# Transformer blocks on one core: row vectors and normalized x through TensorE, attention values as the stationary side, two heads side by side

## The chip, the core and the metric

The kernel runs on one core of a Trainium2 chip. The metric is the device time of one execution in microseconds (us). Engines are named as the profile names them: PE is TensorE's matmul side, PEld its weight loads, DVE VectorE, ACT ScalarE, POOL GpSimd, SP the queue that starts the DMA transfers.

## What is computed

A sequence of 256 tokens of width 1024 in float32 passes through three blocks, cut here to what the change touches:

```python
c_act = silu(c)
for layer in range(2):                          # adaptive layers 0 and 1
    shift, scale, gate = split(c_act @ w_ada[layer] + b_ada[layer], 3)
    h = rms_norm(x, norm_g[layer]) * (1 + scale) + shift
    y = even_mixer(h) if layer == 0 else odd_mixer(h)
    x = x + gate * y
x = rms_norm(x, final_g)

# odd_mixer (layer 1): 16 heads of 64, causal softmax over 256 keys
p = softmax(q @ k.T * scale, causal)
y = (merge(p @ v) * silu(z)) @ w_out

# second block: 8 heads of stick-breaking attention, one of three gated branches
A[t, s] = sigmoid(z_ts) * prod_{s<j<t} (1 - sigmoid(z_tj))
y_a = merge(A @ v) @ w_attn_out
```

The second block goes on with a depthwise convolution branch, a short convolution branch, gates, and a feed-forward layer.

## The kernel before

Everything lives in two token tiles (`tt` 0 and 1) of 128 rows. Each projection is a sum over 8 row blocks of 128 (fewer for the narrow ones). For float32 accuracy at the faster float32r rate, each operand is split into a rounded part and its rest: `split` (line 651) makes the two halves of a weight tile with one copy on ACT and one subtraction on DVE, and `mm3` (line 658) issues three matmuls of 128x512, here called wide matmuls, into an `acc` bank of PSUM. Everything else, scores, values and transposes, is plain float32 and goes to the `m` banks, four of them.

The order of work is written twice. First, `program` records every instruction; a ticker (`after`, `every`) places side work such as attention units between the projection's matmuls. Then `Order.best` and `solve` (lines 271 and 284) list-schedule the recorded instructions with the durations of `cost` (line 508), choose the slots of the pools, and issue all engines' instructions in that order. Each engine then runs its own list strictly in order. `fused` (line 148) keeps the instructions recorded inside it together as one piece of that list.

What the change and the steps below touch:

- **Start.** The condition vector `c` is loaded twice, as columns into `col`, and as a row repeated on 128 partitions into `cb` (line 745; a 512 KB DMA of its own). ACT and DVE apply silu to both. `ada_v` (line 964) multiplies a transposed 512 KB weight tile by `cb` on DVE, summing along the row. For the first two row blocks `ada_pe` (line 971) does this on TensorE, four column tiles of 32 at a time. The results land in `ab`. `rsqrt` makes the norms of x, ACT writes x times its norm into `xn` (line 1005), and `h_t` (line 995) transposes a 128x128 piece of it, applies scale and shift on ACT into `f`, and splits `f` into `hT`. `e1_mm` (line 1020) uses `hT` and the first weights for the first wide matmuls: 12 of 512 columns and 6 of 408 for each of 8 row blocks.
- **Gates.** `gate_rows` (line 1361) turns a column of gate values into a row on all partitions: DVE multiplies the identity by each column (16 tiles over both layers), and TensorE multiplies by `ones`.
- **Layer 1.** `o_unit` (line 1483) works on 4 heads for tt 0 and on 2 for tt 1 through `sm_unit` (line 883): scores, softmax numerators `e`, transposes into `pt`, then `values`: for each head and key block one matmul with `pt` stationary (128x128) and `v` moving (64 columns). That is 48 matmuls. `o_done` divides by the sums, `gated` multiplies by silu(z), `to_lhs` transposes and splits the product.
- **Stick-breaking.** `st_unit` (line 1703) does one head: scores, tanh, a scan on DVE, three transposes, three matmuls for the values, 64 columns moving (24 in all). `st_done` transposes and splits the result, 8 transposes.

Of the kernel before, what the change touches and what calls it, by code (L numbers as in the profile page):

```python
# [21 lines left out]
P = 128  # L22
D = 1024
# [86 lines left out]
_ROWS = [("c", 1024), ("fg", 1024), ("mg", 1024), ("ffg", 1024),  # L110
# [397 lines left out]
def cost(engine, name, writes, reads, kw):  # L508
# [69 lines left out]
def program(ctx: ExitStack, tc: tile.TileContext, found, x_d, wst, rows, cols, rope, w2, out, dbg=None):  # L578
# [167 lines left out]
    for a, b in ((0, 72), (72, NCOL)):  # L746
        nc.sync.dma_start(col[:, a:b], cols[:, a:b])
        if a == 0:
            nc.sync.dma_start(cb, rows[0:1, ROWS["c"][0]:ROWS["c"][1]].to_broadcast([P, D]))
# [7 lines left out]
    ones = const.tile([P, P], F32, name="ones")  # L757
    V.memset(ones, 1.0)
# [124 lines left out]
    def sm_unit(tt, segs, klen, masks, o, den, sink=None):  # L883
# [20 lines left out]
        def turn():  # L904
# [3 lines left out]
            transposes(pt, e.rearrange("p a b -> p (a b)"), nb, s.rearrange("p a b -> p (a b)").rearrange("p (c q) -> p c q", q=P))  # L908

# [451 lines left out]
    def gate_rows(layer, j):  # L1361
# [121 lines left out]
    def o_unit(j, tt, u):  # L1483
        n = 4 if tt == 0 else 2
        segs = []
        for i in range(n):
            h = head(tt, u, i)
            segs.append(([(st["q", j][:, h // 2, tt * P:tt * P + P], st["k", j][h % 2][:, h // 2, 0:P * (tt + 1)])],
                         [st["v", j][:, t, 64 * h:64 * h + 64] for t in range(tt + 1)], h))
        kl = P * (tt + 1)  # L1490
        masks = lambda s: (s[:, :, kl - P:kl], causal[:, None, :].to_broadcast([P, n, P]))
        return sm_unit(tt, segs, kl, masks, lambda sl: get(o1, (j, tt), lambda: bank([P, 8, 64], n="o1"))[:, sl, :],
                       lambda sl: den1[:, j, tt, sl:sl + 1])

    def o_done(j, tt):
# [3 lines left out]
        o = t2([P, 8, 64], n="o")  # L1499
        V.tensor_tensor(o, o1[j, tt], cf[:, :, None].to_broadcast([P, 8, 64]), op=ALU.mult)  # L1500
        o1[j, tt] = o
# [20 lines left out]
    for tt in range(2):  # L1522
        after(1 + tt, lambda tt=tt: gated(o1[0, tt], tt, 0))
# [7 lines left out]
    def mid1():  # L1531
        tk.drain()
        for tt in range(2):
            gated(o1[1, tt], tt, 1)
# [166 lines left out]
    os_ = {}  # L1701

    def st_unit(h):
# [14 lines left out]
        def turn():  # L1718
# [4 lines left out]

            def values():
                o = get(os_, ("p", h // 4), lambda: bank([P, 2, 4, 64], n="os"))
                v = qk["v"][:, :, 64 * h:64 * h + 64]
                PE.matmul(o[:, 0, h % 4, :], at[:, 0:P], v[:, 0, :], start=True, stop=True, skip_group_check=True)
                PE.matmul(o[:, 1, h % 4, :], at[:, P:256], v[:, 0, :], start=True, stop=False, skip_group_check=True)
                PE.matmul(o[:, 1, h % 4, :], at[:, 256:384], v[:, 1, :], start=False, stop=True, skip_group_check=True)
                if h % 4 == 3:  # L1730
                    ob = get(os_, "o", lambda: [t2([P, 8, 64], n="so") for _ in range(2)])
                    for tt in range(2):
                        S.activation(ob[tt][:, h - 3:h + 1, :], o[:, tt], AF.Copy, scale=0.5)
# [4 lines left out]

    ya = new_lhs(4)

    def st_done():
        for tt in range(2):
            to_lhs(ya, os_["o"][tt].rearrange("p h d -> p (h d)"), tt, 0, 4)
# [8 lines left out]
    every(2, 8, [launch(lambda h=h: st_unit(h)) for h in range(8)] + [lambda: None, lambda: None, st_done])  # L1752
# [98 lines left out]
def layout(inputs):  # L1851
# [19 lines left out]
    def pe(v):  # L1871
# [14 lines left out]
        "c": a["c"][0], "fg": a["final_g"], "mg": a["mix_norm_g_2"][0],  # L1886
# [35 lines left out]
```

## Time and profile before

| | |
|---|---|
| median of 3 runs | 759.78 us (757.1 to 760.51) |
| profiled execution, its own time | 761.01 us |
| span of the profile | 759.3 us |
| PE busy | 733.1 us (97%), 3712 instructions |
| PEld busy | 596.4 us (79%) |
| DVE busy | 573.7 us (76%), 1057 instructions |
| ACT busy | 404.1 us (53%), 715 instructions |
| DMA | 148.08 MB, mean 195 GB/s |
| granted TensorE clock | 0.997 |

Busy time of PE is the union of matmuls that overlap in the pipeline, so it is not the work done: a wide matmul lasts 407 ns in the trace, while the next may start much earlier. What a matmul costs in a stream is read from the starts of its neighbours. Nearly all instructions carry line 562, the helper that records them, so groups are told apart by tiles and shapes. A float32 matmul appears as two records (x2 for one matmul), a transpose as one.

### The profile page before, as it was taken

Reading aid. Unit: us, or ns where it says so; the run is one execution under the profiler, and the core shown is the slowest. Engines: PE = TensorE matmul, PEld = TensorE weight load, DVE = VectorE, ACT = ScalarE, POOL = GpSimd, SP = SyncE. Lnnn points to the kernel's source line nnn. Section 1 sums busy time; section 2 is a strip of 40 time slices with the busy share of each in tenths; the row PEclk is TensorE's granted clock in tenths of the full one; section 3 lists DMA queues with packets and bytes.
Section 4 is the critical chain, followed back from the end, with each engine's and each line's share of the span. In section 5 each row is a group of like instructions: output and inputs, shape, how many; then the busy total and the mean of one; then the engine's idle time right before and its main releaser. Section 6 shows DMA issues by size and latency. Waiting matters only on the chain.

```text
span 759.3 us, 10452 instructions
## 1 busy us (share of the span) xinstructions
PE 733.1 (97%) x3712; PEld 596.4 (79%) x3712; DVE 573.7 (76%) x1057; ACT 404.1 (53%) x715; POOL 13.7 (2%) x40
## 2 busy tenths in 40 slices
PE   3999999997999999999999999999999999999998
PEld 1887788786787888878877778878887888888886
DVE  4899899957987564598899999997857555646531
ACT  5565878747454546446455564566445444435420
POOL 1000000000000000001000000000000000000000
PEclk9999999999999999999999999999999999999999
DMA  8998978734684533456532476654747555645101
GB/s 325 400 372 285 368 251 297 236 130 140 210 289 136 196 129 114 148 191 209 182 113 84 139 226 208 206 184 174 250 139 253 191 195 173 214 140 193 57 1 55
DMA packets 43572, 148.08 MB, mean 195 GB/s; under 512 B 6272, under 2 KB 7424, under 8 KB 43520
## 3 DMA queue, kind: packets, MB, share of 16 engines
q1 hardware_dynamic: 43520, 147.41, 56.6%
q8 instruction: 29, 0.48, 0.3%
q14 instruction: 23, 0.19, 0.1%
HBM read 146.34 MB, written 1.05 MB: 194 GB/s over the span
## 4 chain that ended last, share of the span: by engine, by line
PE 76%; DVE 10%; DMA 7%; ACT 5%; issue 1%; SPq 0%; ACTq 0%; DVEq 0%
PE acc L562 65%; PE m L562 11%; DMA k<-in_wst_dram 7%; DVE k L562 5%; DVE kr L562 4%; ACT k L562 3%; ACT kr L562 2%; DVE x L562 1%; SPq L562 0%; DVE tiny L562 0%; DVE ab L562 0%; DVE keepA L562 0%; ACTq L562 0%; DVEq L562 0%
## 5 line engine op out<-in xcount | busy, mean ns | idle before, releaser
L562 PE MATMUL acc<-kr,kr 128*128 128x512 f32 x2520 | 653.7, 407 | 4.0 <-ACT kr L562 3.9
L562 PEld LDWEIGHTS acc<-kr,kr 128*128 128x128 f32 x2520 | 469.0, 190 | 103.2 <-ACT k L562 2.8
L562 DVE TENSOR_TENSOR kr<-k,kr 128x1024 fp32r<-128x1024 f32 (+3 forms) x234 | 265.9, 1151 | 85.8 <-PE acc L562 68.0
L562 ACT ACTIVATE kr<-k 128x1024 fp32r<-128x1024 f32 (+3 forms) x234 | 230.6, 1005 | 147.0 <-PE acc L562 98.1
L562 PE MATMUL m<-identf,k 128*128 128x128 f32 x414 | 97.5, 279 | 5.8 <-DVE k L562 4.8
L562 PE MATMUL m<-k,k 128*128 128x64 f32 (+4 forms) x436 | 75.3, 304 | 11.6 <-DMA k<-in_wst_dram 10.6
L562 PEld LDWEIGHTS m<-k,k 128*128 128x128 f32 (+1 forms) x436 | 67.1, 188 | 22.2 <-issue 12.2
L562 ACT ACTIVATE k<-m 128x512 f32<-128x512 f32 (+6 forms) x115 | 53.3, 471 | 39.7 <-PE m L562 38.3
L562 PEld LDWEIGHTS m<-identf,k 128*128 128x128 f32 x414 | 56.7, 146 | 20.8 <-DVE k L562 6.0
L562 DVE CUSTOM_DVE_ANT_0 k<-k,cb 128x1024 f32<-128x1024 f32 x44 | 53.0, 1216 | 2.4 <-DMA k<-in_wst_dram 2.3
L562 DVE SCALAR_TENSOR_TENSOR k<-k,col,k 128x256 f32<-128x256 f32 x128 | 54.2, 475 | 0.0
L562 ACT ACTIVATE k<-m,tiny 128x128 f32<-128x128 f32 (+1 forms) x80 | 32.9, 423 | 21.6 <-DVE tiny L562 18.9
L562 ACT ACTIVATE kr<-m 128x512 fp32r<-128x512 f32 (+3 forms) x52 | 24.9, 491 | 27.6 <-PE m L562 23.7
L562 DVE TENSOR_TENSOR kr<-m,kr 128x256 fp32r<-128x256 f32 (+2 forms) x44 | 23.8, 552 | 13.0 <-PE acc L562 7.5
L562 DVE TENSOR_REDUCE tiny<-m 128x2 f32<-128x512 f32 (+1 forms) x30 | 20.6, 687 | 7.8 <-PE m L562 7.5
L562 DVE TENSOR_TENSOR k<-k,k 128x512 f32<-128x512 f32 (+5 forms) x42 | 24.5, 591 | 0.3
L562 ACT ACTIVATE k<-acc,rf 128x256 f32<-128x256 f32 x22 | 10.3, 472 | 27.0 <-PE acc L562 26.8
L562 DVE SCALAR_TENSOR_TENSOR k<-acc,rf,k 128x256 f32<-128x256 f32 x22 | 10.5, 482 | 18.7 <-ACT k L562 18.5
L562 ACT ACTIVATE k<-k 128x512 f32<-128x512 f32 (+4 forms) x28 | 14.9, 538 | 13.6 <-DVE k L562 13.5
L562 PE MATMUL m<-kr,kr 128*128 128x408 f32 (+1 forms) x96 | 21.7, 329 | 0.1
L562 DVE TENSOR_TENSOR k<-acc,x 128x512 f32<-128x512 f32 x4 | 2.8, 691 | 22.4 <-PE acc L562 22.4
L562 ACT ACTIVATE k<-m,ab 128x128 f32<-128x128 f32 (+1 forms) x24 | 10.6, 489 | 14.9 <-DVE ab L562 14.9
(111 smaller groups left out, 319.9 us busy)
## 6 DMA issues: line engine op xcount, KB each, us to landing
k<-in_wst_dram SPq DMA_DIRECT2D x266, 512.0 KB, 4.5
k<-in_wst_dram SPq DMA_DIRECT2D x8, 204.0 KB, 8.1
k<-in_rows_dram SPq DMA_DIRECT2D x3, 512.0 KB, 3.5
k<-in_rows_dram SPq DMA_DIRECT2D x6, 256.0 KB, 5.5
x<-in_x_dram SPq DMA_DIRECT2D x2, 512.0 KB, 3.8
out_dram<-k SPq DMA_DIRECT2D x4, 256.0 KB, 2.0
cb<-in_rows_dram SPq DMA_DIRECT2D x1, 512.0 KB, 7.0
k<-in_w_dram SPq DMA_DIRECT2D x2, 128.0 KB, 5.9
```

The costliest lines, as they stand in the source:

```text
L562: self._o.add(self._n, lambda: f(*a, **kw), method, writes, reads, info)
```

## The change

Five edits:

1. silu(c) is computed on the column only. `as_rows` spreads a column to a row on all partitions by a matmul whose stationary side is the column repeated and whose moving side is the identity. Eight such matmuls fill `cb`; the DMA of the row is gone. `gate_rows` uses the same helper in place of the DVE multiplications and `ones`.
2. `h_t` multiplies x by a diagonal matrix of its norms (`dg0`) where it transposed `xn`; `xn` and its two passes on ACT are gone.
3. In layer 1 the values are the stationary side (64 columns), the probabilities move (128 columns), and two heads go to the two halves of the output partitions. The result comes out transposed, so z, times the reciprocal sums, is transposed in its place (`z_turn`, `gated_t`).
4. In stick-breaking the same is done for pairs of heads, 256 and 128 columns moving; `st_done` and its transposes are gone.
5. `cost` has a duration for outputs of 64 partitions.

```diff
-            return (d / 4 + 20.0 if writes[0].ap[0][1] == 32 else d), 210.0, None
+            n = writes[0].ap[0][1]
+            return (d / 4 + 20.0 if n == 32 else d / 2 + 10.0 if n == 64 else d), 210.0, None
...
-            nc.sync.dma_start(cb, rows[0:1, ROWS["c"][0]:ROWS["c"][1]].to_broadcast([P, D]))
...
-    V.tensor_scalar(sc32[:, :, 0], ct, 0.5, None, op0=ALU.mult)
-    ct = t4([P, D], n="ct")
-    S.activation(ct, cb, AF.Tanh, scale=0.5)
-    V.scalar_tensor_tensor(ct, ct, 1.0, cb, op0=ALU.add, op1=ALU.mult)
-    V.tensor_scalar(cb, ct, 0.5, None, op0=ALU.mult)
+    V.tensor_scalar(ct, ct, 0.5, None, op0=ALU.mult)
+    V.tensor_copy(sc32[:, :, 0], ct)
+    def as_rows(p, col):
+        for i in range(p.shape[1]):
+            PE.matmul(p[:, i, :], col[:, i:i + 1].to_broadcast([P, P]), identf, start=True, stop=True, skip_group_check=True)
+    for j in range(2):
+        p = bank([P, 4, P], n="cb")
+        as_rows(p, ct[:, 4 * j:4 * j + 4])
+        copy_act(cb[:, 512 * j:512 * j + 512], p.rearrange("p i n -> p (i n)"))
...
-            PE.transpose(p[:, tt, :], xn[tt][:, k * P:k * P + P], identf)
+            PE.matmul(p[:, tt, :], x[:, tt, k * P:k * P + P], dg0[:, tt, :], start=True, stop=True, skip_group_check=True)
...
-    xn = [t4([P, D], n="xn") for _ in range(2)]
-    ss = tn([P, 2])
+    dg0 = t2([P, 2, P], n="dg")
     for tt in range(2):
-        S.activation(xn[tt], x[:, tt, :], AF.Square, accum_out=ss[:, tt:tt + 1])
-    r = rsqrt(ss, 1.0 / D, 2)
-    for tt in range(2):
-        S.activation(xn[tt], x[:, tt, :], AF.Copy, scale=r[:, tt:tt + 1])
+        V.tensor_scalar(dg0[:, tt, :], identf, rstd_of(x[:, tt, :]), None, op0=ALU.mult)
...
-            dg, p = t2([P, 4, P], n="dg"), bank([P, 4, P], n="pg")
-            for i in range(4):
-                V.tensor_scalar(dg[:, i, :], identf, g[:, i:i + 1], None, op0=ALU.mult)
-                PE.matmul(p[:, i, :], ones, dg[:, i, :], start=True, stop=True, skip_group_check=True)
+            p = bank([P, 4, P], n="pg")
+            as_rows(p, g)
...
+        def values(pt):
+            o = get(o1, (j, tt), lambda: bank([P, 4, P], n="o1"))
+            with od.fused():
+                for i in range(0, n, 2):
+                    for b in range(tt + 1):
+                        for a in range(2):
+                            h = n * u + i + a
+                            PE.matmul(o[64 * a:64 * a + 64, h // 2, :], st["v", j][:, b, 64 * h:64 * h + 64], pt[:, i + a, b, :],
+                                      start=b == 0, stop=b == tt, skip_group_check=True)
...
-        V.tensor_tensor(o, o1[j, tt], cf[:, :, None].to_broadcast([P, 8, 64]), op=ALU.mult)
+        copy_act(o, o1[j, tt])
+    def z_turn(hf, tt, cf):
+        z = zz[hf][tt]
+        V.tensor_tensor(hv(z, 8), hv(z, 8), cf[:, :, None].to_broadcast([P, 8, 64]), op=ALU.mult)
+        p, g = bank([P, 4, P]), t2([P, 4, P], n="g")
+        for i in range(4):
+            PE.transpose(p[:, i, :], z[:, i * P:i * P + P], identf)
+        copy_act(g, p)
+        return g
+    def gated_t(o, g, tt, hf):
+        hi, lo = (a[hf][:, :, tt * P:tt * P + P] for a in oT)
+        V.tensor_tensor(o, o, g, op=ALU.mult)
+        copy_act(hi, o)
+        V.tensor_tensor(lo, o, hi.bitcast(F32), op=ALU.subtract)
...
-                o = get(os_, ("p", h // 4), lambda: bank([P, 2, 4, 64], n="os"))
-                v = qk["v"][:, :, 64 * h:64 * h + 64]
-                PE.matmul(o[:, 0, h % 4, :], at[:, 0:P], v[:, 0, :], start=True, stop=True, skip_group_check=True)
-                PE.matmul(o[:, 1, h % 4, :], at[:, P:256], v[:, 0, :], start=True, stop=False, skip_group_check=True)
-                PE.matmul(o[:, 1, h % 4, :], at[:, 256:384], v[:, 1, :], start=False, stop=True, skip_group_check=True)
+                o = get(os_, h // 4, lambda: bank([P, 2, 256], n="os"))[:, h // 2 % 2, :]
+                with od.fused():
+                    for b, (q0, q1, c) in enumerate(((0, 256, 0), (P, 256, 256))):
+                        for i in range(2):
+                            v = qk["v"][:, b, 64 * (h - 1 + i):64 * (h + i)]
+                            PE.matmul(o[64 * i:64 * i + 64, q0:q1], v, ats[h - 1 + i][:, c:c + q1 - q0], start=b == 0, stop=b == 1, skip_group_check=True)
```

Since the scheduler works with other instructions and another duration, the whole order is solved anew. Three places of it follow. In their rows, `k` are SBUF tiles, `kr` their split halves, `m` and `acc` PSUM banks, `tiny` small columns, and the operands behind the arrow are the moving and the stationary side for a matmul.

DVE, the start, before: `ab` is the shift and scale, the ISA rows on 128x1024 are `ada_v`, `kr_80<-k_109` is the rest of the first `hT`.

```order
L562 TENSOR_TENSOR kr_78<-k_65,kr_77 128x1024
L562 TENSOR_TENSOR ab_182<-m_154,col 128x1
L562 TENSOR_SCALAR ab_182<-m_154,one_180,col 128x1
L562 TENSOR_TENSOR kr_80<-k_109,kr_79 128x256
L562 ISA k_69,ab_182<-k_69,cb 128x1024
L562 ISA ab_182 128x1
```

The same place now:

```order
L563 TENSOR_TENSOR kr_78<-k_65,kr_77 128x1024
L563 ISA k_68,ab_181<-k_68,cb 128x1024
L563 ISA ab_181 128x1
L563 TENSOR_TENSOR ab_181<-ab_181,col 128x1
L563 ISA k_69,ab_181<-k_69,cb 128x1024
L563 ISA ab_181 128x1
L563 TENSOR_TENSOR ab_181<-m_156,col 128x1
L563 TENSOR_SCALAR ab_181<-m_156,one_179,col 128x1
```

Two `ada_v` with their loads now stand ahead of the first row block's shift and scale.

ACT, the start, now: behind the first `f` (`k_111`, which reads `ab`) stands a weight split (`kr_81<-k_71`), and then the first `hT` (`kr_82`). Before, the `hT` copy stood right behind its `f`.

```order
L563 ACTIVATE kr_79<-k_70 128x408
L563 ACTIVATE k_111<-m_154,ab_181 128x256
L563 ACTIVATE kr_81<-k_71 128x1024
L563 ACTIVATE kr_82<-k_111 128x256
L563 ACTIVATE k_112<-m_155,ab_181 128x256
```

PE, values of one unit in layer 1, before: `m_155` is the output bank, `k_119` the transposed probabilities (stationary), `k_63` the values, and wide matmuls stand between.

```order
L562 MATMUL acc_149<-kr_84,kr_79 128x512
L562 MATMUL m_155<-k_63,k_119 128x64
L562 MATMUL acc_148<-kr_92,kr_77 128x512
L562 MATMUL m_155<-k_63,k_119 128x64
L562 MATMUL acc_148<-kr_90,kr_77 128x512
L562 MATMUL m_155<-k_63,k_119 128x64
L562 MATMUL acc_148<-kr_92,kr_78 128x512
L562 MATMUL m_155<-k_63,k_119 128x64
```

Such a unit now:

```order
L563 MATMUL acc_150<-kr_83,kr_99 128x512
L563 MATMUL acc_147<-kr_96,kr_93 128x512
L563 MATMUL m_157<-k_116,k_71 64x128 x4
L563 MATMUL acc_147<-kr_98,kr_93 128x512
L563 MATMUL m_154<-identf,k_109 128x128
```

The four matmuls of a unit stand together, between wide ones; there are 12 such rows of four in layer 1, and four groups of two 64x256 and two 64x128 in stick-breaking.

## Rows read from the trace of the kernel before

**Rows 1.** Busy time by stretches (us; start:end, length, then engines, clock, DMA).

```profile
19.00:57.00 38.00, 38.00 (x173) 31.88 (x171) 34.88 (x74) 22.53 (x42) 1.74 (x4) 1.00 1.00 385
57.00:152.00 95.00, 92.73 (x644) 75.61 (x642) 91.55 (x200) 72.56 (x199) 2.31 (x8) 1.00 0.84 288
220.00:320.00 100.00, 98.40 (x549) 81.60 (x547) 60.31 (x89) 54.78 (x119) 1.89 (x2) 1.00 0.47 161
380.00:494.00 114.00, 112.32 (x553) 91.15 (x552) 113.82 (x224) 61.27 (x89) 0.36 (x3) 1.00 0.50 163
```

**Rows 2.** Waits of TensorE (who for whom: total us, times, longest us).

```profile
PE m L562 <- DMA k<-in_wst_dram: 10.6, 1, 10.6
PE m L562 <- DVE k L562: 4.8, 8, 1.6
```

**Rows 3.** Timeline of TensorE in layer 1 (start us, us, engine, line, operation).

```profile
264.63 0.33 PE L562 MATMUL m<-k,k 128*128 128x64 f32 x2
...
265.09 0.33 PE L562 MATMUL m<-k,k 128*128 128x64 f32 x2
...
266.00 0.33 PE L562 MATMUL m<-k,k 128*128 128x64 f32 x2
...
268.98 0.38 PE L562 MATMUL m<-k,ones 128*128 128x128 f32 x2
...
270.34 0.38 PE L562 MATMUL m<-k,ones 128*128 128x128 f32 x2
```

**Rows 4.** Timeline of TensorE, a run of wide matmuls, then transposes among them.

```profile
355.92 19.31 PE L562 MATMUL acc<-kr,kr 128*128 128x512 f32 x84
375.06 0.28 PE L562 MATMUL m<-identf,k 128*128 128x128 f32 x1
...
396.82 0.27 PE L562 MATMUL m<-identf,k 128*128 128x128 f32 x1
...
397.17 0.27 PE L562 MATMUL m<-identf,k 128*128 128x128 f32 x1
```

**Rows 5.** Timeline of TensorE, column-tiled fours of the compressor.

```profile
76.22 1.50 PE L562 MATMUL acc<-k,k 128*32 128x256 f32 x24
77.65 0.44 PE L562 MATMUL m<-identf,k 128*128 128x128 f32 x2
...
80.54 0.64 PE L562 MATMUL acc<-k,k 128*32 128x256 f32 x8
81.11 0.33 PE L562 MATMUL m<-identf,k 128*128 128x128 f32 x1
81.37 0.64 PE L562 MATMUL acc<-k,k 128*32 128x256 f32 x8
```

**Rows 6.** Timeline of all engines, the first 25 us.

```profile
13.07 1.06 ACT L562 ACTIVATE kr<-k 128x1024 fp32r<-128x1024 f32 x1 [0.69 <-DMA k<-in_wst_dram]
...
15.64 0.27 DVE L562 TENSOR_SCALAR ab<-m,one,col 128x1 f32<-128x1 f32 x1
16.01 0.56 ACT L562 ACTIVATE k<-m,ab 128x256 f32<-128x256 f32 x1 [1.61 <-DVE ab L562]
...
16.61 0.42 ACT L562 ACTIVATE kr<-k 128x256 fp32r<-128x256 f32 x1
...
17.40 1.22 DVE L562 CUSTOM_DVE_ANT_0 k<-k,cb 128x1024 f32<-128x1024 f32 x1
...
18.34 1.20 PE L562 MATMUL acc<-kr,kr 128*128 128x512 f32 x2
...
20.05 4.59 PE L562 MATMUL acc<-kr,kr 128*128 128x512 f32 x10
...
24.46 1.29 PE L562 MATMUL m<-kr,kr 128*128 128x408 f32 x6
```

**Rows 7.** Groups by form (x count | busy us, mean ns | idle before).

```profile
L562 DVE TENSOR_SCALAR k<-identf,ab 128x128 f32<-128x128 f32 x16 | 3.6, 282 | 0.1
...
L562 PEld LDWEIGHTS acc<-k,k 128*32 128x32 f32 x64 | 1.5, 108 | 1.7 <-issue 1.0
```

More of the change, by code (lines that the diff above doesn't have):

```diff
@@ L756, in program @@
     nc.sync.dma_start(rp, rope.rearrange("t p d -> p t d"))
-    ones = const.tile([P, P], F32, name="ones")
-    V.memset(ones, 1.0)
     sel = const.tile([P, 32], F32, name="sel")
@@ L881, in head, with sm_unit @@
         return 2 * i + u if tt == 0 else 4 * (u % 2) + 2 * i + u // 2
-    def sm_unit(tt, segs, klen, masks, o, den, sink=None):
+    def sm_unit(tt, segs, klen, masks, o, den, sink=None, give=None):
         ns = len(segs)
@@ L908, in turn @@
             transposes(pt, e.rearrange("p a b -> p (a b)"), nb, s.rearrange("p a b -> p (a b)").rearrange("p (c q) -> p c q", q=P))
+            if give is not None:
+                return lambda: give(pt.rearrange("p (i b) q -> p i b q", b=kb))
             def values():
@@ L1484, in o_unit @@
         n = 4 if tt == 0 else 2
[L1485 to L1489, printed above, removed]
+        segs = [([(st["q", j][:, h // 2, tt * P:tt * P + P], st["k", j][h % 2][:, h // 2, 0:P * (tt + 1)])], None, h)
+                for h in range(n * u, n * u + n)]
         kl = P * (tt + 1)
         masks = lambda s: (s[:, :, kl - P:kl], causal[:, None, :].to_broadcast([P, n, P]))
-        return sm_unit(tt, segs, kl, masks, lambda sl: get(o1, (j, tt), lambda: bank([P, 8, 64], n="o1"))[:, sl, :],
-                       lambda sl: den1[:, j, tt, sl:sl + 1])
+        def values(pt):
[7 more added lines that the diff above has]
+                                      start=b == 0, stop=b == tt, skip_group_check=True)
+        return sm_unit(tt, segs, kl, masks, None, lambda sl: den1[:, j, tt, sl:sl + 1], give=values)
     def o_done(j, tt):
@@ L1522, in program @@
     for tt in range(2):
-        after(1 + tt, lambda tt=tt: gated(o1[0, tt], tt, 0))
+        after(1 + tt, lambda tt=tt: gated1(0, tt))
     proj("odd31", hT, z_evict(1))
@@ L1699, in v_evict @@
         scaled(get(qk, "v", lambda: t4([P, 2, 512], n="v"))[:, tt, :], acc, tt)
-    os_ = {}
+    os_, ats = {}, {}
+    ya = new_lhs(4)
     def st_unit(h):
@@ L1722, in turn @@
             copy_act(at, z[:, 0:384])
+            ats[h] = at
+            if h % 2 == 0:
+                return lambda: None
             def values():
-                o = get(os_, ("p", h // 4), lambda: bank([P, 2, 4, 64], n="os"))
-                v = qk["v"][:, :, 64 * h:64 * h + 64]
-                PE.matmul(o[:, 0, h % 4, :], at[:, 0:P], v[:, 0, :], start=True, stop=True, skip_group_check=True)
-                PE.matmul(o[:, 1, h % 4, :], at[:, P:256], v[:, 0, :], start=True, stop=False, skip_group_check=True)
-                PE.matmul(o[:, 1, h % 4, :], at[:, 256:384], v[:, 1, :], start=False, stop=True, skip_group_check=True)
+                o = get(os_, h // 4, lambda: bank([P, 2, 256], n="os"))[:, h // 2 % 2, :]
[4 more added lines that the diff above has]
+                            PE.matmul(o[64 * i:64 * i + 64, q0:q1], v, ats[h - 1 + i][:, c:c + q1 - q0], start=b == 0, stop=b == 1, skip_group_check=True)
                 if h % 4 == 3:
-                    ob = get(os_, "o", lambda: [t2([P, 8, 64], n="so") for _ in range(2)])
-                    for tt in range(2):
-                        S.activation(ob[tt][:, h - 3:h + 1, :], o[:, tt], AF.Copy, scale=0.5)
-            return values
-        return turn
[L1739 to L1743, printed above, removed]
+                    b = h // 4
+                    hi, lo = (a[0][:, 2 * b:2 * b + 2, :] for a in ya)
+                    S.activation(hi, os_[b], AF.Copy, scale=0.5)
+                    V.scalar_tensor_tensor(lo, os_[b], 0.5, hi.bitcast(F32), op0=ALU.mult, op1=ALU.subtract)
+            return values
+        return turn
     proj("p3", hT, cfval)
@@ L1751, in program @@
     proj("p2", hT, v_evict)
-    every(2, 8, [launch(lambda h=h: st_unit(h)) for h in range(8)] + [lambda: None, lambda: None, st_done])
+    every(2, 8, [launch(lambda h=h: st_unit(h)) for h in range(8)])
     proj("p5", hT, sc_x)
```

14 lines of the change are left out of this document (8 added, 6 removed).

## The prediction

> **What bounds the kernel now.** First the busy times by stretches [rows 1]: PE is at work in all of 19 to 57 us, in 92.7 of 95 us after that, 98.4 of 100 in layer 1 (220 to 320) and 112.3 of 114 where stick-breaking stands (380 to 494). DVE is as full as PE in two of these stretches, 91.6 of 95 and 113.8 of 114, and has room in layer 1, 60 of 100. Then PE's waits [rows 2]: 10.6 us at the start for the first weights, and behind that the largest is 4.8 us in eight waits for DVE. So PE sets the pace, and an edit is worth what it takes out of PE's stream, at the pace at which instructions follow each other and not at their durations.
>
> Those paces come from the timeline. A run of 84 wide matmuls takes 375.06 - 355.92 = 19.14 us, 0.228 each [rows 4]. A transpose and a wide matmul together take 0.35 [rows 4], so a transpose costs 0.12. In layer 1 three values matmuls of 64 columns, each with a wide one, take 266.00 - 264.63 = 1.37, 0.457 a pair, so one of them costs 0.229; with 128 columns it is (270.34 - 268.98) / 3 - 0.228 = 0.225 [rows 3]. Twice the columns cost nothing: the price is not the moving side. That is what the change can use.
>
> Two heads side by side are not in this trace; the nearest rows are the compressor's column tiles, four matmuls of 32 output partitions and 256 columns [rows 5]. One such four, up to the next instruction, takes 81.11 - 80.54 = 0.57, three in a row take 77.65 - 76.22 = 1.43: another four costs 0.43, and 0.14 goes on the way out. From the transpose behind a four to the next four it is 0.26, less 0.12 for the transpose leaves 0.14 on the way in. So tiles of one round run side by side, a round of 128 columns should take half of 0.43, 0.215, and every return to full-width work costs 0.28.
>
> **The change, part by part.**
>
> *Values of layer 1.* Before, 48 matmuls at 0.229: 11.0 us. Now 12 units, each two rounds and one change of mode: 2 x 0.215 + 0.28 = 0.71, together 8.5. That is **-2.5 us**. If the change of mode hides beside the wide matmuls, a unit costs 0.43 and the gain is 5.8; if the two heads run one after the other, a unit costs 4 x 0.215 + 0.28 = 1.14, and it is a loss of 2.7. I take the first, since the fours are the same kind of instruction.
>
> *Stick-breaking.* Before, 24 matmuls at 0.229: 5.5 us. Now four groups of a round of 256, a round of 128 and a change: 0.43 + 0.215 + 0.28 = 0.925, together 3.7: **-1.8 us** (-2.9 to +0.8 by the same bounds). The 8 transposes of `st_done` go: **-1.0 us**. DVE is full there, but what fills it are convolution steps that the scheduler ranks last and that are needed late.
>
> *Layer 1, z turned in place of the output.* Transposes are as many as before, 16. DVE has as many large operations as before, ACT gets two copies more in each of four places. The chain from z to the split grows by a DVE and an ACT operation. It is covered by wide matmuls on the first half of the heads: in the new order 16 wide matmuls, some 3.6 us, stand between the last transpose of z and the first matmul that reads its half. Nothing is put down; without that cover it would be about 1 us once.
>
> *h_t.* 16 transposes become float32 matmuls of 128 columns. Half of them are issued before the first wide matmul, the other 8 in the stream, at 0.225 instead of 0.12: **+0.8 us**.
>
> *Gates.* PE has the same 16 matmuls. DVE loses 16 operations of 0.282 us [rows 7]. The 8 of layer 1 are worth nothing, DVE has room there. The 8 of layer 0, 2.3 us, fall where DVE is full and some of PE's waits are for it: between 0 and -2.3, I take **-1.0 us**.
>
> *Start.* The row DMA was 512 KB in front of all weights; at the 385 GB/s of [rows 1] that is 1.36 us, by which every weight lands earlier. ACT loses three passes over 1024 columns. But the new order on DVE puts two `ada_v` and their loads ahead of the first shift and scale. The first `ada_v` began at 17.40, as its tile landed [rows 6]; that tile now lands 1.36 us earlier, and the second one 1.36 us behind it, again at 17.40. From there, with the second `ada_v` (1.22) and its readout, the 0.16 and 0.27 of shift and scale, `f` (0.56), the split that ACT now has ahead (1.06) and the `hT` copy (0.42) [rows 6] it is 21.3 until the first wide matmul, where it was 18.34. That is not 3 us lost: before, ten wide matmuls from 20.05 took 24.46 - 20.05 = 4.4 us, 0.44 each, twice their pace elsewhere, the pace of the lower of the two clock levels (1.2 and 2.4 GHz), after a start in which PE had worked in pieces. The first row block, 12 wide and 6 narrower ones, was done at 25.7. Now it would be 25.3 at full pace (12 x 0.228 and 6 x 0.19 from 21.3), and 28.8 if all 18 run at the lower level: between -0.4 and +3.1. On the side of the weights and of DVE the start is 1.36 us early. PE and DVE are both nearly full up to 57 us, so either may decide; I take **0**, and keep -1.4 and +3.1 as ends.
>
> The sum is -2.5 - 1.8 - 1.0 + 0.8 - 1.0 = -5.5 us. Against the profiled execution, 761.0, it gives 755.5; the median before is 1.2 us below that execution, so 759.8 - 5.5 = **754.3 us**. The order is solved anew everywhere, which can move some us either way with no edit to blame.
>
> **A rule that speaks against it.** The weight loads of the fours take 0.108 us each in the profile [rows 7], and still a further four costs no more than 0.43 [rows 5], so they run under the matmuls. The Trainium skill, TensorE: Matmul & The Clock Gate, Part 3 (packing small matmuls), says that a weight load overlaps with matmuls in flight only if it goes to another row group; here all tiles use all rows. The fours disagree with that. By that rule loads would stand bare, which is part of rival 2.
>
> **Rivals.**
>
> 1. *The start costs, and DVE's relief is not felt.* The first wide matmuls come at 21.3, all at the lower level, and PE never catches up: +3.1, and the gates give 0: 754.3 + 3.1 + 1.0 = 758.4. For it: PE is at work in every us from 19 to 57 [rows 1]. Against: DVE has less to do and its weights earlier.
> 2. *Two heads gain nothing, and it gets slower.* The place is the 16 tiled groups of layer 1 and stick-breaking. If the halves of 64 run one after the other, layer 1 loses 2.7 instead of gaining 2.5, and stick-breaking 0.8 instead of gaining 1.8: 754.3 + 7.8 = 762.1. If only the loads stand bare, each of four load steps of a group adds 0.108, 16 x 0.43 = 6.9: 761.2. It decides as soon as a group in layer 1 takes over 0.92, four times 0.229. Against it: the fours of 32.
> 3. *The change of mode hides.* Then 16 x 0.28 = 4.5 more is gained: 749.8. For it: at two of the groups a transpose stands next to them that may fill the gap. Against it: the fours had transposes beside them too and showed 0.28.
>
> **How the numbers follow.** The forecast has 0.60, with its own range 751 to 758; rival 1 has 0.20, rival 2 0.08, rival 3 0.12. Half a per cent, about what a measurement of this kernel can tell from no change, is 3.8 us: faster means below 756.0, slower above 763.6. The forecast lies below 756.0 in three quarters of its cases (0.45), rival 3 always (0.12), rival 1 rarely (0.01): faster 0.58. Rival 2 passes 763.6 only together with a late start, and new order may add to it: slower 0.05. The rest, 0.37, is no change. The range for 8 in 10 reaches from the edge of rival 3, 749.5, over rival 1 up to 760.0, and leaves out rival 2 and what lies beyond either end.
>
> **What would show it.** In the changed profile a group of four 128x64 tiles between wide matmuls should take about 0.7 us from its start to the next group's or wide matmul's start, less what that one costs; over 0.92 is rival 2, under 0.5 rival 3. Matmuls of 64 moving columns in layer 1 and stick-breaking should be gone, and eight transposes with them. The first weights should land near 9.2 instead of 10.6 us; the first wide matmul should start near 21 us, and the time at which the first row block is done tells rival 1 from the forecast. DVE should be some 4 us less busy. The prediction is wrong if PE's stream from 220 to 494 holds the gain and the end does not move: then a wait of DVE or a weight tile has taken its place, most likely between 57 and 190 us, or if the start alone loses more than 3 us.

## The result and the profile after

The changed kernel takes 751.4 us in the median (749.2 to 753.1, four runs), beside 759.7 for the kernel before: ratio 0.990, 95% interval 0.986 to 0.993. That is 8.3 us less; the forecast was 5.5 less, with 749.5 to 760.0 as its range. The profiled execution took 751.05 us, where that of the kernel before took 761.01. Executions of one kernel differ with the TensorE clock that they were granted: the changed kernel's four, with mean clocks of 1.000, 0.998, 0.997 and 0.995, took 749.2, 751.1, 751.7 and 753.1 us.

Busy times by stretches, changed kernel, the same four stretches as [rows 1]:

```profile
19.00:57.00 38.00, 37.27 (x188) 32.38 (x187) 35.70 (x72) 23.89 (x46) 1.94 (x5) 1.00 0.99 379
57.00:152.00 95.00, 92.51 (x640) 75.75 (x640) 91.15 (x193) 72.80 (x199) 2.12 (x8) 1.00 0.87 303
220.00:320.00 100.00, 100.00 (x558) 78.02 (x557) 65.92 (x92) 58.93 (x126) 1.90 (x2) 1.00 0.51 178
380.00:494.00 114.00, 112.49 (x540) 88.83 (x540) 113.27 (x203) 59.80 (x82) 0.35 (x3) 1.00 0.53 176
```

PE is still what bounds: it is now busy in all 100 us of layer 1's stretch. Waits of TensorE in the changed kernel, as in [rows 2]:

```profile
PE m L563 <- DVE k L563: 12.7, 6, 9.9
PE acc L563 <- ACT kr L563: 2.6, 2, 1.8
...
PE m L563 <- DVE ab L563: 1.2, 1, 1.2
```

The longest of the six waits for DVE, 9.9 us, is the start: PE now waits for DVE's diagonal instead of for weights. The other five come to 2.8 us, where eight came to 4.8 before [rows 2]. DVE's multiplications of the identity, 16 in [rows 7] for the gates, are down to four, none of them a gate, and DVE is busy for 569.5 us instead of 573.7, the 4 us that the forecast named:

```profile
L563 DVE TENSOR_SCALAR k<-identf,tiny 128x128 f32<-128x128 f32 x4 | 1.1, 286 | 0.1
```

**Where the time went.** Both kernels issue 2520 wide matmuls, so the start of the n-th one is a common clock. It splits the run into layer 0 (up to number 420), layer 1 (to 840), the part with stick-breaking (to 1344) and the rest, up to the start of the last one:

```
                 layer 0   layer 1   stick   rest
before           201.1     137.2     138.0   278.9
changed kernel   199.2     132.1     135.1   278.8
difference        -1.9      -5.1      -2.9    -0.1
```

The forecast, put in the same columns, had -0.2 (start 0, `h_t` +0.8, gates -1.0), -2.5 and -2.8. Stick-breaking came out as said; layer 1 and layer 0 gave more.

**The groups in layer 1.** Timeline of TensorE in the changed kernel, one group of two rounds between wide matmuls:

```profile
228.03 0.84 PE L563 MATMUL acc<-kr,kr 128*128 128x512 f32 x3
228.81 0.66 PE L563 MATMUL m<-k,k 128*64 128x128 f32 x8
229.39 0.50 PE L563 MATMUL acc<-kr,kr 128*128 128x512 f32 x1
```

The four matmuls are 8 records, two passes each. The next wide matmul starts 229.39 - 228.81 = 0.58 us after the group's first, and the wide matmuls on either side of it take about 0.1 us more than their 0.228. Over the ten groups that stand among wide matmuls and transposes alone, and with those taken off at 0.228 and 0.12, a group costs 0.77 us on average (0.70 to 0.88). The forecast was 0.71.

**The start.** Timeline of all engines in the changed kernel, the lines that answer to [rows 6]:

```profile
9.94 1.22 PE L563 MATMUL m<-k,x 128*128 128x128 f32 x4 [9.94 <-DVE k L563]
...
10.96 2.95 PE L563 MATMUL m<-identf,tiny 128*128 128x128 f32 x16
...
11.83 1.06 ACT L563 ACTIVATE kr<-k 128x1024 fp32r<-128x1024 f32 x1 [3.82 <-DMA k<-in_wst_dram]
...
15.80 1.22 DVE L563 CUSTOM_DVE_ANT_0 k<-k,cb 128x1024 f32<-128x1024 f32 x1 [1.66 <-ACT k L563]
...
17.14 1.22 DVE L563 CUSTOM_DVE_ANT_0 k<-k,cb 128x1024 f32<-128x1024 f32 x1
...
18.73 0.56 ACT L563 ACTIVATE k<-m,ab 128x256 f32<-128x256 f32 x1 [0.63 <-DVE ab L563]
...
20.59 3.05 PE L563 MATMUL acc<-kr,kr 128*128 128x512 f32 x12 [0.73 <-ACT kr L563]
...
23.48 1.26 PE L563 MATMUL m<-kr,kr 128*128 128x408 f32 x6
...
24.58 0.63 PE L563 MATMUL acc<-kr,kr 128*128 128x512 f32 x2
```

ACT's split, which began at 13.07 before, begins at 11.83, so the weights are 1.24 us earlier (forecast 1.36). Two `ada_v` stand ahead of the first shift and scale, and the first wide matmul starts at 20.59 (forecast 21.3, before 18.34). Its 12 wide ones take 23.48 - 20.59 = 2.9 us, 0.24 each, where they took 0.44 before; the first row block is done at 24.7 (25.7 before).

### The profile page after: what moved, and what is told of

Read it like the earlier page. It is cut to its first block, busy times and chain, and to the rows that moved or that the text cites. A ratio compares the mean times of both kernels' runs of the same rounds, so it can differ in the third digit from the quotient of the medians.

```text
span 749.3 us, 10467 instructions
## 1 busy us (share of the span) xinstructions
PE 726.4 (97%) x3720; PEld 589.0 (79%) x3720; DVE 569.5 (76%) x1048; ACT 404.6 (54%) x718; POOL 13.7 (2%) x40
## 4 chain that ended last, share of the span: by engine, by line
PE 84%; DVE 7%; ACT 4%; DMA 3%; issue 1%; SPq 0%; DVEq 0%; ACTq 0%
PE acc L563 71%; PE m L563 13%; DVE k L563 4%; DMA k<-in_wst_dram 3%; DVE kr L563 3%; ACT k L563 2%; ACT kr L563 2%; SPq L563 0%; DVE tiny L563 0%; DVE x L563 0%; DVE ab L563 0%; DVEq L563 0%; ACT tiny L563 0%; ACTq L563 0%; DVE keepA L563 0%
## 5 line engine op out<-in xcount | busy, mean ns | idle before, releaser
L563 PE MATMUL acc<-kr,kr 128*128 128x512 f32 x2520 | 644.5, 406 | 2.6 <-ACT kr L563 2.6
L563 DVE TENSOR_TENSOR kr<-k,kr 128x1024 fp32r<-128x1024 f32 (+3 forms) x238 | 269.2, 1144 | 89.4 <-PE acc L563 65.0
L563 PE MATMUL m<-identf,k 128*128 128x128 f32 x390 | 94.4, 274 | 3.3 <-DVE k L563 2.2
L563 ACT ACTIVATE k<-m 128x512 f32<-128x512 f32 (+7 forms) x119 | 56.6, 483 | 45.2 <-PE m L563 43.1
L563 PE MATMUL m<-k,k 128*128 128x64 f32 (+6 forms) x420 | 62.4, 302 | 1.3 <-ACT k L563 1.0
L563 PEld LDWEIGHTS m<-identf,k 128*128 128x128 f32 x390 | 53.3, 143 | 13.2 <-ACT k L563 3.0
L563 PEld LDWEIGHTS m<-k,k 128*128 128x128 f32 (+2 forms) x420 | 49.1, 168 | 12.1 <-issue 4.5
L563 ACT ACTIVATE kr<-m 128x256 fp32r<-128x256 f32 (+3 forms) x48 | 22.5, 485 | 20.2 <-PE m L563 12.8
L563 PE MATMUL m<-kr,kr 128*128 128x408 f32 (+1 forms) x96 | 24.7, 339 | 0.2
L563 ACT ACTIVATE k<-k 128x512 f32<-128x512 f32 (+4 forms) x28 | 15.0, 543 | 14.1 <-DVE k L563 13.9
L563 PE MATMUL m<-k,x 128*128 128x128 f32 x64 | 10.6, 292 | 11.7 <-DVE k L563 10.5
L563 DVE TENSOR_TENSOR kr<-m,kr 128x256 fp32r<-128x256 f32 (+2 forms) x38 | 19.6, 530 | 2.7 <-ACT kr L563 1.9
```

The source lines that it names most:

```text
L563: self._o.add(self._n, lambda: f(*a, **kw), method, writes, reads, info)
```

## The experiments

Each was timed beside the kernel before on its chip; ratios are to that, with 95% intervals. The changed kernel's is 0.990 [0.986, 0.993].

### One part undone at a time

**Start undone.** The row DMA of c, its silu in rows, `xn` and the transposes come back.

```diff
-            PE.matmul(p[:, tt, :], x[:, tt, k * P:k * P + P], dg0[:, tt, :], start=True, stop=True, skip_group_check=True)
+            PE.transpose(p[:, tt, :], xn[tt][:, k * P:k * P + P], identf)
```

> The changed kernel with its start undone: c comes as a row by DMA again, x is scaled by its norm on ScalarE and turned by transposes (both as before); gates, layer 1 and stick-breaking stay changed. The changed kernel stood at 751.4 us, 0.9895 of the kernel before. Theory A (each part gives what its own edit removes): the two traces differ by 1.9 us at the 420th wide matmul, 2.3 us behind at the first and 1.3 us ahead at the 84th, so undoing the start gives back 1.9 us, 753.3. Theory B (most of what the forecast missed is a re-solved order, not an edit): layer 0 keeps a part of its gain, 751.4 to 752.4, or moves by as much either way in stages that this edit does not touch. The forecast on record had this part at 0 (between 3.1 lost and 1.4 gained): 751.4.

Measured: 753.2 us, 0.991 [0.989, 0.993]; layer 0 took 198.0 us, no longer than in the changed kernel (199.2). The 84th wide matmul came at 49.8, as before, and the 1.1 us by which the changed kernel is ahead there is not there any more at the 420th. So 753.3 is not borne out by the place: layer 0 gives nothing back. The comparison is blurred by the clock, though. The profile of the changed kernel has a stretch of some 3.4 us in layer 0 in which the granted clock is 0.50, the level of 1.2 GHz; the profile with the start undone has none. Busy times in it (the clock is the third number from the end):

```profile
176.90:180.20 3.30, 3.30 (x10) 2.65 (x9) 2.64 (x13) 1.20 (x3) 0.39 (x1) 0.50 0.00 0
```

Wide matmuls start 0.43 us apart there instead of 0.23, so such a stretch costs about 1.6 us (an estimate: 3.4 us hold 8 of them where 15 would go). Without it layer 0 would have given back some 0.4 us.

**Layer 1 undone.** `o_unit`, `o_done` and the gating as before.

> The changed kernel with layer 1's attention as before: 48 value matmuls of 64 columns, their output evicted and gated in rows and turned by transposes. Theory A: 12 units of 4 x 0.229 = 0.92 us instead of groups that measured 0.77 us, so 1.8 us more, 753.2 (the forecast had 2.5: 753.9). Theory B: the two traces part by 3.7 us between the 420th and the 756th wide matmul; if the order carries the rest, undoing the part moves the time by another amount than 1.8, up to 3.7 (755.1), and the trace shows it as other waits, not in the value matmuls.

Measured: 751.1 us, 0.988 [0.986, 0.990], no slower than the changed kernel. But the stages show two effects: layer 1 took 134.8 us, 2.7 more than in the changed kernel, and layer 0 took 196.6, 2.7 less, in an order that from the 84th wide matmul on is another one. Of these 2.7 us about 1.6 are the clock: no stretch at 0.50 is recorded in this profile's layer 0. The total alone would have said that the edit is worth nothing.

**Stick-breaking undone.**

> The changed kernel with stick-breaking as before: 24 value matmuls of 64 columns, output evicted in rows, 8 transposes. Theory A: 4 x (1.375 - 1.0) = 1.5 us for the values and 8 x 0.12 = 1.0 for the transposes, together 2.5 us more, 753.9. Theory B: the traces part by 4.2 us between the 840th... 1344th wide matmul, of which 1.4 us before 378 us is no term of this edit; the run would move by up to 4 us, 755.4, or by less than 1.

Measured: 753.1 us, 0.991 [0.989, 0.993]; the stage took 137.8 us instead of 135.1. In this kernel PE's order up to the 924th wide matmul is that of the changed kernel, so the 2.7 us of the stage are the edit's own. Theory A holds here.

**Gates undone.** The diagonals on DVE and the matrix of ones come back.

```diff
-            as_rows(p, g)
+            for i in range(4):
+                V.tensor_scalar(dg[:, i, :], identf, g[:, i:i + 1], None, op0=ALU.mult)
+                PE.matmul(p[:, i, :], ones, dg[:, i, :], start=True, stop=True, skip_group_check=True)
```

> The changed kernel with the gates' rows made as before: VectorE multiplies the unit matrix by each of 16 gate columns (16 x 0.282 us) and TensorE multiplies a matrix of ones by it. The forecast's term: layer 0's eight stand on VectorE where TensorE waits for it, worth 1.0 us of their 2.3; layer 1's eight cost nothing: 752.4. Theory A': VectorE's relief is not felt at all: 751.4. Theory A'': all of layer 0's is felt: 753.7. Theory B: an order re-solved for an edit that takes nothing from TensorE moves the time by a us or more either way.

Measured: 753.5 us, 0.991 [0.989, 0.994]. Layer 0 took 200.7 us, 1.5 more than in the changed kernel. But it holds two stretches at the lower clock where the changed kernel holds one, and that alone is about 1.6 us:

```profile
18.30:21.60 3.30, 3.27 (x11) 2.54 (x11) 2.65 (x7) 3.27 (x8) 0.00 (x0) 0.50 1.04 400
178.70:182.00 3.30, 3.30 (x9) 2.59 (x9) 2.53 (x12) 2.82 (x5) 0.34 (x1) 0.50 0.19 73
```

The total is nearest to theory A'', but the place does not show it: three executions of this kernel with a granted clock of 0.997 took 751.1, 751.9 and 753.2 us, the changed kernel's with 0.997 took 751.7.

The four undoings give back 1.8, 0, 1.7 and 2.1 us by their medians, 5.6 of 8.3; by the intervals of the ratios none of the four is clear of the changed kernel. That raised the suspicion that the order of the kernel before happened to be a poor one.

### The same instructions in another order

**The kernel before in two other orders.**

```diff
-SLACK, ROUNDS = {"k4": 0, "kr": 0, "acc": 0, "k2": 0, "m": 0, "tiny": 0}, 7
+SLACK, ROUNDS = {"k4": 0, "kr": 0, "acc": 0, "k2": 0, "m": 0, "tiny": 0}, 11
```

> The kernel before, with the same instructions in another order: the scheduler is let search 11 rounds in place of 7 and picks another of its orders. Undone one at a time, start, layer 1, stick-breaking and gates gave back about 1.8, 0, 1.7 and 2.1 us, 5.6 of 8.3 to 8.7, so some 3 us belong to no edit alone. Theory B (order): the order of the kernel before holds two waits of TensorE that no changed order shows, 2.1 us for ACT's kr at 185 us and 1.6 us for DVE at 232 us; another order of the same instructions loses most of them, 756 to 757.5. Theory A (the edits themselves, or their working together): 759.7, and waits of the same size stand there again.

> The kernel before in a third order (the scheduler's search cut to 4 rounds). Theory B: 756 to 757.5, or anything from 755 to 762 if orders scatter by some us either way; no wait of 1.5 us or more at 185 and 232 us. Theory A: 759.7.

Measured: 759.1 us, 1.000 [0.999, 1.002], and 761.5, 1.005 [1.003, 1.006]. Theory B, that a lucky order makes the gain, falls: no order of the old instructions comes near. Half of its premise falls too. The wait at 185 us is gone in both, but that at 232 us is not chance. TensorE's waits from 215 to 245 us, in the kernel before:

```profile
PE m L562 <- DVE k L562: 1.6, 1, 1.6
```

in its first other order:

```profile
PE m L562 <- DVE k L562: 2.3, 1, 2.3
```

and in its second:

```profile
PE m L562 <- DVE k L562: 1.4, 1, 1.4
```

**The changed kernel in another order.**

```diff
-            return (d / 4 + 20.0 if n == 32 else d / 2 + 10.0 if n == 64 else d), 210.0, None
+            return (d / 4 + 20.0 if n == 32 else d), 210.0, None
```

> The changed kernel in another order: the scheduler's price for a matmul tile of 64 columns is put back to that of a full one; the instructions are the same. Theory B: the time scatters by the order alone, between 749 and 755; theory A: 751.4 within 1 us.

Measured: 753.2 us, 0.993 [0.992, 0.995]. Its stick-breaking stage lost 3.2 us (138.3 instead of 135.1), more than half of it in one new wait. TensorE's waits from 420 to 432 us:

```profile
PE m L563 <- ACT k L563: 1.7, 1, 1.7
PE m L563 <- DVE k L563: 0.3, 1, 0.3
```

Behind that wait the clock was low. TensorE from 429.2 to 432.5 us:

```profile
429.20:432.50 3.30, 3.30 (x12) 0.50 0.00 0
```

In the changed kernel no stretch at 0.50 is recorded in this stage. So the wait of the new order is 1.7 of the 3.2 us, and the clock about 1.6; that the wait brought the lower clock about is not shown.

### Do two heads run side by side?

**Loops reversed**, everything else in place:

```diff
-                for i in range(0, n, 2):
-                    for b in range(tt + 1):
-                        for a in range(2):
+                for a in range(2):
+                    for i in range(0, n, 2):
+                        for b in range(tt + 1):
```

> The changed kernel, in the same order of everything, except that inside each group of layer 1's value matmuls the loop over the two heads is the outermost: the halves of 64 no longer alternate, so that two neighbours go to the same half. If it is the alternation that lets two heads run side by side, each round that stood at 0.22 us becomes 0.43, and a group grows from 0.59 to up to 1.02 us: 12 x 0.43 = 5.2 us more, 756.6; if only the neighbours at the switch run side by side, about half, 754. If the gain comes from fewer or shorter instructions and not from running side by side (rival 2 of the forecast, seen from the other side): 751.4, group unchanged.

Measured: 751.6 us, 0.991 [0.990, 0.992]. The group of above, timeline of TensorE:

```profile
228.73 0.67 PE L563 MATMUL m<-k,k 128*64 128x128 f32 x8
229.33 0.50 PE L563 MATMUL acc<-kr,kr 128*128 128x512 f32 x1
```

0.60 us to the next start, as good as the 0.58 of the changed kernel. So alternating is not what matters. The run could not yet say whether halves run side by side or 64 stationary columns are cheap in themselves.

**Both heads of a group in one half.** The number, shapes and order of the instructions stay; a group's four matmuls now all go to the lower half of the output partitions, or all to the upper.

```diff
+                            q, w = (u, i + a) if n == 4 else (u % 2, u // 2 * 2 + a)
-                            PE.matmul(o[64 * a:64 * a + 64, h // 2, :], st["v", j][:, b, 64 * h:64 * h + 64], pt[:, i + a, b, :],
+                            PE.matmul(o[64 * q:64 * q + 64, w, :], st["v", j][:, b, 64 * h:64 * h + 64], pt[:, i + a, b, :],
```

> The changed kernel in the same order of everything, but in layer 1 both heads of a group write into the same half of the output partitions (one group the lower half, the next the upper), so the heads come out in another order than the reference's. Same count, same shapes, same number of loads. If the gain in layer 1 comes from two halves running side by side (which the reversed loops left possible), a round of 0.109 us per pair of passes becomes two, and a group grows from 0.59 to about 4 x 0.22 + 0.15 = 1.0 us: 12 x 0.43 = 5.2 us more than the changed kernel, ratio 0.996. If 64 stationary columns are cheaper by themselves, with no running side by side, the groups stay at 0.59 and the ratio at 0.990.

Measured: 756.0 us, 0.995 [0.993, 0.997]. The same group, timeline of TensorE:

```profile
228.72 1.09 PE L563 MATMUL m<-k,k 128*64 128x128 f32 x8
229.73 0.50 PE L563 MATMUL acc<-kr,kr 128*128 128x512 f32 x1
```

1.01 us, 0.43 more, in all twelve groups: 5.1 us. The layer took 137.1 us, 5.0 more than the changed kernel's 132.1, and as much as before the change. This is rival 2 of the prediction made real: a group costs 1.19 where it put 1.14, and the whole gain of the layer is gone. So two halves do run side by side, worth 5 us here.

### The change in halves

**Gates alone**, on the kernel before.

> The kernel before with one edit: the gates' rows come from TensorE by a spread column against the unit matrix, so that VectorE loses its 16 multiplications of 0.28 us; start, layer 1 and stick-breaking as before. Forecast on record: 1.0 us gained, all in layer 0, ratio 0.9987. From the run with the gates undone: 2 to 2.7 us, ratio 0.9965, all ahead of the 420th wide matmul. If DVE's relief also clears the wait for it at 232 us, up to 4.5 us, ratio 0.994. If the relief only pays together with the other edits: 1.0 within 0.002.

Measured: 758.5 us, 0.9986 [0.9970, 1.0002], 1.1 us less, with zero just inside the interval. Layer 0 took 198.6 us, and TensorE's wait near 230 us is smaller. Its waits for DVE from 215 to 245 us:

```profile
PE m L563 <- DVE k L563: 1.0, 1, 1.0
```

**Start and gates**, with layer 1 and stick-breaking as before, and **layer 1 and stick-breaking**, with start and gates as before.

> The kernel before with start and gates changed, layer 1 and stick-breaking as before: one half of the change. The forecast's terms for this half: start 0, products with the diagonal +0.8, gates -1.0, together -0.2 us, ratio 1.000. If the parts simply add as the single undoings measured them (start 1.8, gates 2.1): 3.9 us, ratio 0.995; if what the trace shows in layer 1 beside its own edit (2.3 us) belongs to this half: 5 us, ratio 0.9935.

> The other half: the kernel before with layer 1 and stick-breaking changed, start and gates as before. The forecast's terms: -2.5 - 1.8 - 1.0 = -5.3 us, ratio 0.993. By the undoings (0 and 1.7): 1.7 us, ratio 0.998. By the stages of the traces (1.9 in layer 1, 2.8 in stick-breaking): 4.7 us, ratio 0.994. If the two halves add up, the gains of this run and of the run before make 8.3 us together.

Measured: 755.1 us, 0.9945 [0.9925, 0.9965], and 750.0, 0.987 [0.985, 0.990]. The halves gain 4.2 and 9.6 us, 13.7 together, where the whole gains 8.3: they overlap by some 5 us. The second half alone is at least as fast as the whole change; that it is faster is not shown, the intervals overlap.

All stages, from one profile each, in us. The column "clock" is an estimate of what layer 0 lost by the stretches in which a granted clock of 0.50 is recorded, at 1.6 us for 3.4:

```
                     layer 0  clock  layer 1  stick   ratio
before                201.1    1.6    137.2   138.0
  other order 1       198.5    1.6    137.6   138.0   1.000
  other order 2       202.0    1.6    136.5   137.7   1.005
gates alone           198.6    1.6    136.9   137.9   0.999
start, gates          196.9    1.6    135.5   137.9   0.9945
layer 1, stick        200.0    1.6    132.1   134.9   0.987
changed kernel        199.2    1.6    132.1   135.1   0.990
  start undone        198.0    0      133.5   135.1   0.991
  gates undone        200.7    3.2    132.8   135.6   0.991
  layer 1 undone      196.6    0      134.8   134.7   0.988
  stick undone        197.9    1.6    133.3   137.8   0.991
  other order         196.8    1.6    133.1   138.3   0.993
  loops reversed      199.3    3.2    132.7   135.0   0.991
  one half            199.2    3.2    137.1   135.1   0.995
```

## Why the prediction was right, and what it missed

What bounds, the mechanism and the sign held. PE sets the pace, the matmuls of 64 moving columns cost as much as wider ones, and what the change takes from PE's stream comes off the end, with 0.1 us of drift after the last changed place. The sum was 2.8 us short, and that it was no further off is in part luck, since errors cancel: the values of layer 1 gave 0.7 us less than forecast, z and a wait without a term 3.0 more. By terms:

- **Values of layer 1, -2.5.** 12 groups at 0.77 instead of four matmuls at 0.229 each (0.92) give -1.8. The change of mode was mis-sized: two rounds take 0.43, so it costs 0.34 and not 0.28. The mechanism is shown by the run with one half.
- **z turned, 0.** This term was wrong. At the end of layer 1 the kernel before turned its last outputs in one piece that had to wait, and its eight transposes stood bare. Timeline of TensorE, before:

```profile
332.76 1.25 PE L562 MATMUL m<-identf,k 128*128 128x128 f32 x8 [0.53 <-DVE k L562]
```

  After, z takes the sums of the softmax and not the heads' values, so its transposes are spread among wide matmuls, one by one:

```profile
330.19 0.27 PE L563 MATMUL m<-identf,k 128*128 128x128 f32 x1
330.22 0.48 PE L563 MATMUL acc<-kr,kr 128*128 128x512 f32 x1
330.54 0.27 PE L563 MATMUL m<-identf,k 128*128 128x128 f32 x1
```

  From the 756th to the 840th wide matmul all six kernels with the old layer 1 took 22.45 to 22.49 us, and the eight with the new one 20.9 to 22.2, 21.1 in the changed kernel: **-1.4 us**. All values matmuls lie ahead of the 756th in both kernels, so this is apart from them; no run undoes the turning of z alone. The prediction looked for a longer chain from z, and found it covered, but did not ask what the old chain had cost.
- **The wait for DVE at 232 us.** It was in [rows 2] as the longest wait, 1.6 us, and no term took it up. It shows in all four kernels with start and layer 1 as before (1.6, 2.3, 1.4 and 1.0 us), and is absent in the four that have one of the two as before. With both changed it is absent in four kernels and back with 1.0 and 0.4 us in two that keep the changed kernel's order up to there (stick-breaking undone, loops reversed), so it is near its edge. It is one loss that either of two parts of the change takes away for the most part. Layer 1 shows it: the edit of layer 1 is worth 4.2 us with the old start (137.0 in the mean of four, 132.8 of two) and 2.4 with the new one (135.2 of two, 132.8 of five, the run with one half left out). This is the part of the overlap that has a place. The trace says what DVE was late for. In the kernel before, the operation that released TensorE stood on DVE behind an `ada_v` that had waited 1.07 us for its weight tile:

```profile
232.53 1.23 DVE L562 CUSTOM_DVE_ANT_0 k<-k,cb 128x1024 f32<-128x1024 f32 x1 [1.07 <-DMA k<-in_wst_dram]
...
233.68 0.69 DVE L562 TENSOR_TENSOR k<-k,k 128x512 f32<-128x512 f32 x1
...
234.42 0.88 PE L562 MATMUL m<-identf,k 128*128 128x128 f32 x6 [1.60 <-DVE k L562]
```

  An `ada_v` that waited for its tile stands a little ahead in five of the six kernels with this wait (1.07, 1.46, 0.52, 1.16 and 0.77 us), and not in the one with the gates alone. So it is for the most part a wait for weights, and TensorE meets it by coming early, too: with stick-breaking undone layer 0 was 1.3 us shorter than in the changed kernel, and layer 1 1.2 us longer. No run moved that tile alone.
- **Stick-breaking, -1.8, and its transposes, -1.0.** -2.8 forecast, -2.7 with PE's order unchanged up to the stage, -2.9 in the two traces. Within the term, the groups cost about 1.0 us instead of 0.925, one of them here, with 0.80 to the next start and the rest lost by its neighbours:

```profile
415.69 0.87 PE L563 MATMUL m<-k,k 128*64 128x256 f32 x8
416.49 1.21 PE L563 MATMUL acc<-kr,kr 128*128 128x512 f32 x4
```

- **Gates, -1.0, and start, 0, with `h_t` +0.8.** These are smaller than what layer 0 scatters by. Four profiles with the same order of it (the changed kernel, stick-breaking undone, loops reversed, one half) give 197.9 to 199.3, other orders 196.6 to 202.0. Part of the scatter is the clock; with the column "clock" taken off, the four give 197.6, 196.3, 196.1 and 196.0, and the changed kernel is last because its first wide matmul came at 20.59, in the other three at 19.2 to 19.6. By totals the gates are worth 1.1 us alone, with zero in the interval, and 2.1 in the undoing, of which the clock may be a good part. In layer 0, kernels with the new gates are shorter in the mean by 2.1 us among those with the old start and by 2.8 among those with the new one, by about 1.3 and 1.4 with the clock's estimate taken off. So the forecast's bounds (0 to -2.3) hold, and its -1.0 may well be right, but it is not shown apart from the scatter. Start with `h_t` is within 0.5 us of nothing in layer 0, and about 1.3 us gained with the clock taken off; the +0.8 was not seen apart. (The forecast's 25.3 for the first row block at full pace comes to 25.2 by its own terms; 24.7 was measured.)
- **Rivals.** Rival 1 fell: the first row block was earlier, not later. Its other half, that DVE's relief is not felt, is not excluded by the runs on the gates. Rival 2 has its point of decision at 0.92, the groups cost 0.77. Rival 3 had a group below 0.5; entry and exit cost their 0.34 in nearly all of them.

In layer 1 these sizes, 1.8 and 1.4 and the wait's 1.6, make 4.8 of the 5.1 us by which the two profiles differ there; with 2.8 for stick-breaking and the 1.9 of layer 0, which is measured and not explained, it is 9.5 of their 10.0. The medians differ by 8.3, since the profiled execution of the kernel before lay 1.2 us above its median. What stays open is the rest of the overlap, some 3 us: start and gates gain 4.2 us on the kernel before and nothing on top of the other half, and of that only the wait at 232 us was found. The clock is not the rest: at the same granted clock of 0.998, start and gates took the kernel before from 759.4 to 754.6 us in the mean, and 751.1 with them stands beside 750.5 without them where the other half is in (one execution each). With a scatter of 1 to 3 us in layer 0 by order and by run, it can't be said whether there is more behind it.

On the rule that was weighed (the Trainium skill, TensorE: Matmul & The Clock Gate, Part 3: a weight load overlaps only where the row group differs): the run with one half sends all loads and passes of a group to one and the same tile, and the group with its 8 loads and 8 passes takes 1.01 us. Timeline of the weight loads in the group of above, first with one half, then in the changed kernel:

```profile
228.71 0.85 PEld L563 LDWEIGHTS m<-k,k 128*64 128x64 f32 x8 [0.35 <-ACT k L563]
```

```profile
228.80 0.42 PEld L563 LDWEIGHTS m<-k,k 128*64 128x64 f32 x8 [0.35 <-ACT k L563]
```

With one half the loads fill 228.71 to 229.56 and the passes begin at 228.72, so they run through each other without another row group, and rival 2's second form had no ground here. The trace does not agree with the rule. In the changed kernel the 8 loads take half as long, 0.42 us, since the two halves load side by side as well.

## What to carry to other kernels

A float32 matmul of 64 moving columns cost here what one of 128 did (0.229 and 0.225 us); where many of them stand in the stream, make the narrow side stationary and put two on the two halves of the output, and count some 0.34 us for every return to full width, so that by this sum longer groups are worth more. Ask of an edit not only what its new chain costs but what the old one did: a step that no longer depends on the late result can be spread beside other work, which here gave 1.4 us beside the 1.8 of the packing in the same layer. And where a scheduler solves the order anew, an undone part has to be read stage by stage, since the total mixes it with a scatter of its own size; and the granted clock of a stage has to be read before two profiles of it are compared.

## What was not expected

- **The halves need not alternate.** With all matmuls of one half issued ahead of those of the other, a group took 0.60 us instead of 0.58. The second half's matmuls evidently start before the first half's queued ones are done.
- **The first wide matmuls at full pace.** They took 0.24 us each in the changed kernel and 0.44 before, and the prediction put the slower pace down to the lower clock level. The granted clock seems to deny it, as it reads 1.00 in both. Busy times by stretches, before:

```profile
10.00:19.00 9.00, 7.54 (x46) 3.79 (x47) 5.06 (x8) 5.29 (x9) 0.00 (x0) 1.00 1.03 409
19.00:25.00 6.00, 6.00 (x19) 4.94 (x18) 3.81 (x10) 3.40 (x8) 0.00 (x0) 1.00 1.03 403
```

  after:

```profile
10.00:19.00 9.00, 7.59 (x66) 6.38 (x67) 5.49 (x20) 3.73 (x7) 0.00 (x0) 1.00 1.03 409
19.00:25.00 6.00, 5.27 (x28) 4.51 (x27) 5.29 (x11) 4.60 (x9) 0.00 (x0) 1.00 1.03 398
```

  But the trace of the kernel before holds no record of the clock ahead of 24.5 us, and that of the changed kernel none ahead of 13.0; where there is no record, the number reads 1.00 all the same. The pace decides. In the run with the loops reversed the clock is on record at that place, at 0.50, the level of 1.2 GHz, and its first 12 wide matmuls take 24.93 - 19.64 = 5.3 us, 0.44 each, the pace of the kernel before. Its busy times, then its timeline of TensorE:

```profile
19.00:25.00 6.00, 5.36 (x13) 4.20 (x14) 5.68 (x10) 3.67 (x8) 0.00 (x0) 0.50 1.04 398
19.64 5.49 PE L563 MATMUL acc<-kr,kr 128*128 128x512 f32 x12 [0.73 <-ACT kr L563]
24.93 1.66 PE L563 MATMUL m<-kr,kr 128*128 128x408 f32 x6
```

  So the prediction read the slow pace rightly. TensorE was busy for as long ahead of 19 us in both kernels, but in the changed one it worked from 9.94 to 13.9 us without a break. What raised the clock earlier was not tried by itself. Nor does it always stay up: loops reversed has the changed kernel's order here, and its clock was back at 0.50 from about 19 us.
